# Pinning the side loads and sums of the adaLN weights in their written order, and moving all matmul operands to multiples of 256 bytes

## The chip, the cores and the metric

One core of a Trainium2 chip runs one program. The metric is the device time of the whole kernel in microseconds (us), median of three runs. Engines: PE (TensorE, matrix products), DVE (VectorE), ACT (ScalarE), POOL (GpSimd) and SP, which here only issues transfers from HBM. Each engine runs its own row of instructions strictly in order and waits on semaphores for the others. TensorE's clock is granted at one of two levels, 2.4 GHz (shown as 1.00) or 1.2 GHz.

## What is computed

Two layers over 512 positions of width 1024 (one sequence). Layer 0 is retention (4 heads, 64-position chunks), layer 1 is chunked attention (16 heads). Cut to what matters here:

```python
cond = silu(c)
for i in range(2):
    mod = cond @ ada_w[i] + ada_b[i]                 # 1024 -> 3072
    shift, scale, gate = split(mod, 3)
    h = rms_norm(x, norm_g[i]) * (1 + scale) + shift
    out = retention(h) if i == 0 else attention(h)   # projections in and out of the mixer
    x = x + gate * out
```

So `shift` and `scale` of layer 0 are needed before its first projection, its `gate` before the first output projection, and all of layer 1's `mod` only when layer 0 is over.

## The kernel before, in words

**Matrix products.** All operands are 4-byte values. Every operand of a large product is held as two parts, `hi` and `lo` (`hi` by ACT, `lo = raw - hi` by DVE), and each product is three matmuls, hi*hi, hi*lo and lo*hi: lines 231 to 233 (`nat_mm`) and 239 to 241 (`tr_mm`). Most are 128x128 stationary against 512 moving columns. A projection is a `Chunk` of 512 output columns: it loads two halves of 512 weight rows (1 MB, `raw`, two buffers), splits them (`whi`, `wlo`, two buffers each), and runs four units of 12 matmuls per half. Of the stationary operand and the moving one, one is a slice of the weight tiles, the other a slice of `hT` (the normed input), or, in an output projection (`po_r`, `po_a`), of the tiles `yh`, `yl`.

**The adaLN vectors.** `cond @ ada_w` is not done on PE: the weights come transposed, a block of 128 output features is a 128x1024 tile, and DVE multiplies it with `cond` and sums along the row (`ada_dot`, line 124; its trace name is CUSTOM_DVE_ANT_0). Shift and scale of layer 0 (16 blocks) are done in the first stage by `ada_256`. The other 32 blocks, 8 for layer 0's gate and 24 for layer 1, are called **side blocks**: `side_load` (line 589, 512 KB each, into two buffers of tag `ada`) and `side_dot`. The program hangs them on units of the projections: the first eight every second unit, the rest every third or fourth unit, the load four units ahead of its sum. When four sums are there, `ada_finish` adds the bias, and for the gate spreads it with two small PE products (`gp`) into `gates`, which POOL multiplies into the output weights (line 219).

**What sets the order.** The code is traced in the order written, but a scheduler then lays out each engine's row: an instruction whose inputs are early may move ahead of others. Side loads and sums have few inputs, so it moves them forward. The names used below: `rv`, `rqk`, `rg` are layer 0's projections for values, queries and keys, and the SiLU gate; `vl`, `ql`, `kl` low parts made from PSUM; `rt` rotary products; `st` scores, `ro` their product with the values, `ss` transposes for the norm of `ro`, which need `sq` summed by POOL (line 550); `dec` the decay table, loaded through POOL's queue; `ang`, `n` the rotary angles.

**Addresses.** Each tile has a fixed byte offset in every partition. In the built program before, the weight tiles `whi`, `wlo` and the tiles `hTh`, `hTl` start 128 bytes past a multiple of 256; `yh`, `yl` of most output projections, `qh`, `kh`, `pth`, `vh` and their low parts start at multiples of 256. So 2,736 of the 512-column matmuls take both operands at 128 past, 720 take one at 128 past and one at a multiple (384 of `po_r`, 288 of the first three `po_a`, 48 of the first half of `aqk0`), and the products of scores and values take both at multiples. The last output projection (`po_a` with `yh_last`) has both at 128 past.

Of the kernel before, what the change touches and what calls it, by code (L numbers as in the profile page):

```python
# [11 lines left out]
F32 = mybir.dt.float32  # L12
# [3 lines left out]
ALU = mybir.AluOpType  # L16

P = 128
S = 512
D = 1024  # L20
# [22 lines left out]
def hybrid_trunk_kernel(  # L43
# [20 lines left out]
    nc = tc.nc  # L64
    PS = bass.MemoryType.PSUM

    cp = ctx.enter_context(tc.tile_pool(name="cp", bufs=1))
# [3 lines left out]
    sp = ctx.enter_context(tc.tile_pool(name="sp", bufs=4))  # L71
# [20 lines left out]
    nc.vector.memset(ones, 1.0)  # L92
    ones_r = cp.tile([P, P], F32R, name="ones_r")
    nc.vector.tensor_copy(ones_r, ones)
    mhalf = cp.tile([P, 8], F32, name="mhalf")
    nc.gpsimd.memset(mhalf, -0.5)

    with tc.high_priority():
# [15 lines left out]
    def rstd_of(ss, n, w):  # L114

        ms = sp.tile([P, w], F32, tag="ms", name="ms")
        nc.gpsimd.tensor_scalar(ms, ss, 1.0 / n, EPS, ALU.mult, ALU.add)
        rs = sp.tile([P, w], F32, tag="rs", name="rs")
        nc.gpsimd.tensor_tensor(rs, ms, mhalf[:, :w], ALU.pow)
        return rs  # L120


    def ada_dot(raw, layer, block):
        nc.vector.tensor_tensor_reduce(  # L124
            raw, raw, cond, 1.0, 0.0, ALU.mult, ALU.add, mod[:, layer, block : block + 1]
        )

    def ada_finish(layer, b0, n):

        m, b = mod[:, layer, b0 : b0 + n], bt[:, layer, b0 : b0 + n]  # L130
        if b0 < NK:
            nc.vector.tensor_tensor(sh[:, layer, b0 : b0 + n], m, b, ALU.add)
            return
        nc.vector.tensor_tensor(m, m, b, ALU.add)
        if b0 < 2 * NK:
            g0 = b0 - NK
            nc.vector.scalar_tensor_tensor(
                gs[:, layer, g0 : g0 + n], m, 1.0, ng[:, layer, g0 : g0 + n], ALU.add, ALU.mult
            )
            return  # L140

        ps = pa.tile([P, n, P], F32, tag="pa", name=f"gp_{layer}_{b0}")
        for j in range(n):
            diag = np_.tile([P, P], F32, tag="diag", name=f"diag_{layer}_{b0 + j}", bufs=2)
            nc.vector.tensor_scalar(diag, ident, m[:, j : j + 1], None, ALU.mult)
            nc.tensor.matmul(ps[:, j, :], ones, diag, start=True, stop=True)
        g0 = (b0 - 2 * NK) * P
        nc.scalar.activation(
            gates[layer][:, g0 : g0 + n * P], ps.rearrange("p a b -> p (a b)"), AF.Copy
        )  # L150
# [12 lines left out]
    def norm_rows(t, tag, scalar=False):  # L163

        xn, ss = [], sp.tile([P, 2], F32, tag="ss", name=f"ss_{tag}_{t}")
        for half in range(2):
            xh = np_.tile([P, 512], F32, tag="p", name=f"xn_{tag}_{t}_{half}", bufs=6)
            nc.scalar.activation(
                xh, xs[t][:, half * 512 : (half + 1) * 512], AF.Square,
                accum_out=ss[:, half : half + 1],  # L170
            )
            xn.append(xh)
        s1 = sp.tile([P, 1], F32, tag="s1", name=f"s1_{tag}_{t}")
        nc.vector.tensor_tensor(s1, ss[:, 0:1], ss[:, 1:2], ALU.add)
        rs = rstd_of(s1, D, 1)
        for half in range(2):
            src = xs[t][:, half * 512 : (half + 1) * 512]
            if scalar:
                nc.scalar.activation(xn[half], src, AF.Copy, scale=rs)
            else:  # L180
                nc.vector.tensor_scalar(xn[half], src, rs, None, ALU.mult)
        return xn

    def norm_tile(layer, t):
        xn = norm_rows(t, layer)
        tsl = slice(t * P, (t + 1) * P)
        for half in range(2):
            ps = pa.tile([P, 4, P], F32, tag="pa", name=f"hp_{layer}_{t}_{half}")
            for k in range(4):
                nc.tensor.transpose(ps[:, k, :], xn[half][:, k * P : (k + 1) * P], ident)  # L190
            h = np_.tile([P, 4, P], F32, tag="nat", name=f"h_{layer}_{t}_{half}")
            for k in range(4):
                kt = half * 4 + k
                g1, s1 = gs[:, layer, kt : kt + 1], sh[:, layer, kt : kt + 1]
                if half == 0:
                    nc.vector.tensor_scalar(h[:, k, :], ps[:, k, :], g1, s1, ALU.mult, ALU.add)
                else:
                    nc.scalar.activation(h[:, k, :], ps[:, k, :], AF.Identity, bias=s1, scale=g1)
            ksl = slice(half * 4, half * 4 + 4)
            nc.scalar.activation(hT["h"][:, ksl, tsl], h, AF.Copy)  # L200
            nc.vector.tensor_tensor(hT["l"][:, ksl, tsl], h, f32(hT["h"][:, ksl, tsl]), ALU.subtract)
# [146 lines left out]
    with tc.tile_pool(name="st", bufs=1) as st:  # L348
        xT = st.tile([P, NK, S], F32, name="xT")

        def ada_256(b0):
            raw = st.tile([P, 2, D], F32, tag="ada", name=f"ada_0_{b0}", bufs=6)
            nc.sync.dma_start(
                raw, ada_t[0, b0 * P : (b0 + 2) * P, :].rearrange("(b p) k -> p b k", p=P)
            )
            for j in range(2):
                ada_dot(raw[:, j, :], 0, b0 + j)
            ada_finish(0, b0, 2)

        def norm_x():  # L360
            for t in range(NT):
                nc.sync.dma_start(xs[t], x[t * P : (t + 1) * P, :])
            for t in range(NT):
                xn = norm_rows(t, 0, t == 3)
                for half in range(2):
                    ps = pa.tile([P, 4, P], F32, tag="pa", name=f"hp_0_{t}_{half}")
                    for k in range(4):
                        nc.tensor.transpose(ps[:, k, :], xn[half][:, k * P : (k + 1) * P], ident)
                    nc.scalar.activation(
                        xT[:, half * 4 : half * 4 + 4, t * P : (t + 1) * P], ps, AF.Copy  # L370
                    )
# [42 lines left out]
    with ExitStack() as l0:  # L414
# [171 lines left out]

        def side_load(layer, block):
            raw = np_.tile([P, D], F32, tag="ada", name=f"ada_{layer}_{block}", bufs=2)
            nc.sync.dma_start(raw, ada_t[layer, block * P : (block + 1) * P, :])
            held[layer, block] = raw  # L590

        def side_dot(layer, block):
            ada_dot(held.pop((layer, block)), layer, block)
            if block % 4 == 3:
                ada_finish(layer, block - 3, 4)

        held = {}
        blocks = [(0, 16 + b) for b in range(8)]
        blocks += [(1, b) for b in (*range(8, 16), *range(8), *range(16, 24))]
        for z, (layer, block) in enumerate(blocks):  # L600
            u = 2 + 2 * z if z < 8 else 20 + (z - 8) * 7 // 2
            at(max(u - 4, 0), side_load, layer, block)
            at(u, side_dot, layer, block)
# [300 lines left out]
```

## Time and profile before

| What | Value |
|---|---|
| Time, median of 3 runs | 1009.23 us (1007.08 to 1010.11) |
| Time of the profiled execution | 1008.13 us |
| Its span, first to last instruction | 1006.4 us |
| PE busy | 961.0 us (95%) |
| DVE busy | 595.7 us (59%) |
| ACT busy, POOL busy | 373.1 us (37%), 183.5 us (18%) |
| Mean granted clock of PE over the span | 0.980 |

How to read it: PE is busy nearly all the time, so its row is the kernel's length wherever it does not wait; the share over the span hides that the first fifth is another stage. The profile's windows show, for a stretch of time, each engine's busy time, the granted clock of PE, and what the DMA engines moved. The list of waits says who waited for whom. A timeline row is start, length, engine, line, operation, output and inputs, count, and in brackets the idle time of that engine just before it and what ended it. A matmul's length in the trace includes its way through the array, so matmuls that follow each other overlap; what counts is the distance of their starts.

### The profile page before, as it was taken

How to read it: one execution, taken by the hardware profiler on the slowest of the kernel's cores; microseconds unless marked ns; L12 is line 12 of the kernel's file. 1: busy time of each engine (PE TensorE's matmuls, PEld its weight loads, DVE VectorE, ACT ScalarE, POOL GpSimd, SP SyncE). 2: the span in 40 equal slices, each digit the busy share in tenths (PEclk: the TensorE clock that was granted, in tenths of full speed). 3: DMA queues.
4: the chain of work that ended last, by engine and by line, in shares of the span. 5: the costliest groups of instructions: out<-in, count | busy, mean ns of one | idle time of the engine just before them, and what ended most of it. 6: DMA issues, size and time to landing. Idle time of an engine off the chain costs nothing.

```text
span 1006.4 us, 11781 instructions
## 1 busy us (share of the span) xinstructions
PE 961.0 (95%) x4528; PEld 800.4 (80%) x4528; DVE 595.7 (59%) x1023; ACT 373.1 (37%) x785; POOL 183.5 (18%) x169
## 2 busy tenths in 40 slices
PE   3879978999999999999999999999999999999997
PEld 2657766888888888888788888888888888888886
DVE  5989879435742474577345465735467346556674
ACT  6223222223222332426443454325534244543441
POOL 3000222006000203331200152002330012104410
PEclk8889988999999999999999999999999999999999
DMA  9868662231223122232133322232323231232202
GB/s 350 307 199 294 226 188 78 95 106 63 84 95 119 49 84 84 84 126 84 40 107 95 95 95 85 63 103 76 95 78 111 85 94 58 81 95 95 95 1 84
DMA packets 70296, 111.76 MB, mean 111 GB/s; under 512 B 11888, under 2 KB 36512, under 8 KB 70240
## 3 DMA queue, kind: packets, MB, share of 16 engines
q1 hardware_dynamic: 58256, 103.29, 30.7%
q0 software_dynamic: 10832, 5.62, 2.0%
q10 hardware_dynamic: 1152, 2.10, 0.6%
q8 instruction: 35, 0.57, 0.2%
q14 instruction: 21, 0.17, 0.0%
HBM read 108.83 MB, written 2.10 MB: 110 GB/s over the span
## 4 chain that ended last, share of the span: by engine, by line
PE 82%; DVE 10%; DMA 5%; issue 1%; ACT 1%; POOL 1%; SPq 0%; DVEq 0%; POOLq 0%
PE pm_aqk L231 6%; PE pm_aqk L233 6%; PE pm_aqk L232 6%; DVE ada L124 4%; DMA ada<-in_ada_t_dram 4%; PE as L723 3%; PE ao L763 3%; PE po_a L231 3%; PE po_a L233 3%; PE po_a L232 3%; PE pm_av L231 3%; PE pm_av L232 3%; PE pm_av L233 3%; PE po_r L231 3%; PE po_r L232 3%; PE po_r L233 3%
## 5 line engine op out<-in xcount | busy, mean ns | idle before, releaser
L231 PE MATMUL pm_aqk<-whi_aqk,hTh 128*128 128x512 f32 x256 | 102.0, 399 | 0.0
L233 PE MATMUL pm_aqk<-whi_aqk,hTl 128*128 128x512 f32 x256 | 100.5, 393 | 0.0
L232 PE MATMUL pm_aqk<-wlo_aqk,hTh 128*128 128x512 f32 x256 | 100.4, 392 | 0.0
L124 DVE CUSTOM_DVE_ANT_0 ada<-ada,cond 128x1024 f32<-128x1024 f32 x48 | 62.7, 1328 | 12.6 <-DMA ada<-in_ada_t_dram 12.6
L219 POOL TENSOR_TENSOR raw_r<-raw_r,gate 128x2048 f32<-128x2048 f32 x8 | 38.0, 4750 | 142.1 <-DMA raw_r<-in_ret_w_out_dram 89.3
L223 DVE TENSOR_TENSOR wlo_aqk<-raw_aqk,whi_aqk 128x2048 fp32r<-128x2048 f32 x16 | 41.0, 2562 | 30.4 <-ACT whi_aqk L222 30.4
L231 PE MATMUL pm_rv<-whi_rv,hTh 128*128 128x512 f32 x128 | 51.7, 409 | 7.6 <-ACT hTh L306 4.0
L233 PEld LDWEIGHTS pm_aqk<-whi_aqk,hTl 128*128 128x128 f32 x256 | 48.1, 188 | 10.2
L239 PE MATMUL pm_rqk<-hTh,whi_rqk 128*128 128x512 f32 x128 | 52.1, 411 | 4.2 <-DVE vl L307 4.2
L231 PEld LDWEIGHTS pm_aqk<-whi_aqk,hTh 128*128 128x128 f32 x256 | 48.1, 188 | 9.6
L232 PEld LDWEIGHTS pm_aqk<-wlo_aqk,hTh 128*128 128x128 f32 x256 | 48.2, 188 | 9.2
L231 PE MATMUL po_r<-whi_r,yh 128*128 128x512 f32 x128 | 51.4, 404 | 4.1 <-DVE x L327 4.1
L732 ACT ACTIVATE p<-p,nm 128x128 f32<-128x128 f32 (+1 forms) x64 | 35.9, 563 | 49.5 <-DVE nm L730 48.4
L241 PE MATMUL pm_rqk<-hTh,wlo_rqk 128*128 128x512 f32 x128 | 50.9, 403 | 2.3 <-DVE wlo_rqk L223 2.3
L240 PE MATMUL pm_rqk<-hTl,whi_rqk 128*128 128x512 f32 x128 | 52.2, 408 | 0.0
L726 DVE CUSTOM_DVE_ANT_0 p<-as,br 128x128 f32<-128x128 f32 (+1 forms) x64 | 30.4, 486 | 36.8 <-PE as L723 33.7
L232 PE MATMUL po_r<-wlo_r,yh 128*128 128x512 f32 x128 | 51.4, 402 | 0.0
L233 PE MATMUL po_r<-whi_r,yl 128*128 128x512 f32 x128 | 51.4, 401 | 0.0
L232 PE MATMUL pm_rv<-wlo_rv,hTh 128*128 128x512 f32 x128 | 50.8, 397 | 0.0
L239 PE MATMUL pm_ag<-hTh,whi_ag 128*128 128x512 f32 x128 | 50.7, 398 | 0.0
L711 POOL DMA_DIRECT2D br<-in_att_bias_dram x16 | 13.4, 839 | 203.7 <-DVE nm L730 168.5
L240 PE MATMUL pm_ag<-hTl,whi_ag 128*128 128x512 f32 x128 | 50.5, 394 | 0.0
(199 smaller groups left out, 2544.3 us busy)
## 6 DMA issues: line engine op xcount, KB each, us to landing
ada<-in_ada_t_dram SPq DMA_DIRECT2D x32, 512.0 KB, 4.6
raw_aqk<-in_att_w_in_dram SPq DMA_DIRECT2D x32, 512.0 KB, 4.7
ada<-in_ada_t_dram SPq DMA_DIRECT2D x8, 1024.0 KB, 14.1
raw_rg<-in_ret_w_in_dram SPq DMA_DIRECT2D x8, 1024.0 KB, 5.1
raw_r<-in_ret_w_out_dram SPq DMA_DIRECT2D x8, 1024.0 KB, 5.0
raw_ag<-in_att_w_in_dram SPq DMA_DIRECT2D x8, 1024.0 KB, 5.3
raw_av<-in_att_w_in_dram SPq DMA_DIRECT2D x8, 1024.0 KB, 5.3
raw_a<-in_att_w_out_dram SPq DMA_DIRECT2D x8, 1024.0 KB, 5.1
```

The source lines that it names most:

```text
L124: nc.vector.tensor_tensor_reduce(raw, raw, cond, 1.0, 0.0, ALU.mult, ALU.add, mod[:, layer, block : block + 1])
L219: nc.gpsimd.tensor_tensor(raw, raw, scale.unsqueeze(1).broadcast_to([P, k1 - k0, width]), ALU.mult)
L223: nc.vector.tensor_tensor(lo, raw, f32(hi), ALU.subtract)
L231: nc.tensor.matmul(ps, a_h, wh[:, k, :], start=first and k == 0, stop=False)
L232: nc.tensor.matmul(ps, a_h, wl[:, k, :], start=False, stop=False)
L233: nc.tensor.matmul(ps, a_l, wh[:, k, :], start=False, stop=last and k == 3)
L239: nc.tensor.matmul(ps, wh[:, k, csl], h, start=first and k == 0, stop=False)
L240: nc.tensor.matmul(ps, wh[:, k, csl], l, start=False, stop=False)
L241: nc.tensor.matmul(ps, wl[:, k, csl], h, start=False, stop=last and k == 3)
L723: nc.tensor.matmul(ps[:, :w0], a[:, qsl], b[:, :w0], start=z == 0, stop=z == 2)
L726: nc.vector.tensor_tensor_reduce(p[:, :w], ps[:, :w], br[:, S - w :], 1.0, -3.0e38, ALU.add, ALU.max, mx)
L732: nc.scalar.activation(p[:, :w], p[:, :w], AF.Exp, bias=nm, accum_out=sm)
```

## The change

Three kinds of lines change. `keep_in_program_order` adds an edge, without a semaphore, from the instruction that was traced just before on the same engine: the side load may not be placed ahead of the transfer written before it on SP, the side sum not ahead of the DVE instruction written before it. Other instructions remain free to move past them. Two small tiles are made larger, `mhalf` (8 to 40 columns) and `s1` (1 to 16 columns, of which column 0 is used); what lies behind them in a partition moves by 128 bytes. In the built program every matmul operand then starts at a multiple of 256 bytes.

```diff
-    mhalf = cp.tile([P, 8], F32, name="mhalf")
+    mhalf = cp.tile([P, 40], F32, name="mhalf")
...
     def ada_dot(raw, layer, block):
-        nc.vector.tensor_tensor_reduce(
+        return nc.vector.tensor_tensor_reduce(
             raw, raw, cond, 1.0, 0.0, ALU.mult, ALU.add, mod[:, layer, block : block + 1]
         )
...
-        s1 = sp.tile([P, 1], F32, tag="s1", name=f"s1_{tag}_{t}")
-        nc.vector.tensor_tensor(s1, ss[:, 0:1], ss[:, 1:2], ALU.add)
-        rs = rstd_of(s1, D, 1)
+        s1 = sp.tile([P, 16], F32, tag="s1", name=f"s1_{tag}_{t}")
+        nc.vector.tensor_tensor(s1[:, 0:1], ss[:, 0:1], ss[:, 1:2], ALU.add)
+        rs = rstd_of(s1[:, 0:1], D, 1)
...
         def side_load(layer, block):
             raw = np_.tile([P, D], F32, tag="ada", name=f"ada_{layer}_{block}", bufs=2)
-            nc.sync.dma_start(raw, ada_t[layer, block * P : (block + 1) * P, :])
+            tc.keep_in_program_order(
+                nc.sync.dma_start(raw, ada_t[layer, block * P : (block + 1) * P, :])
+            )
             held[layer, block] = raw

         def side_dot(layer, block):
-            ada_dot(held.pop((layer, block)), layer, block)
+            tc.keep_in_program_order(ada_dot(held.pop((layer, block)), layer, block))
             if block % 4 == 3:
                 ada_finish(layer, block - 3, 4)
```

The instructions are the same, but their order on every engine changes in layer 0. First place: DVE's row up to the first `vl`, the low part of the values, which frees the PSUM tile that PE needs for `rqk_2`. `ada_20` to `ada_22` are side blocks. Before:

```order
L436 TENSOR_SCALAR n_468<-ang 128x512
L124 ISA ada_21_740,mod<-ada_21_740,cond 128x1024
L124 ISA mod 128x1
L437 TENSOR_SCALAR n_468<-n_468 128x512
L439 SCALAR_TENSOR_TENSOR ang<-n_468,ang 128x512
L124 ISA ada_22_799,mod<-ada_22_799,cond 128x1024
...
L439 SCALAR_TENSOR_TENSOR ang<-n_468,ang 128x512
L307 TENSOR_TENSOR vl_491<-pm_rv_0_277,vh_490 128x512
```

With the change, the same place on DVE:

```order
L307 TENSOR_TENSOR hTl_112<-h_7_401,hTh_111 128x512
L429 CAST posf<-posi 128x512
L431 TENSOR_SCALAR ang<-posf,tiny 128x512
L436 TENSOR_SCALAR n_468<-ang 128x512
L437 TENSOR_SCALAR n_468<-n_468 128x512
L439 SCALAR_TENSOR_TENSOR ang<-n_468,ang 128x512 x2
L440 TENSOR_SCALAR n_469<-ang 128x512
L307 TENSOR_TENSOR vl_491<-pm_rv_0_277,vh_490 128x512
```

No side sum stands ahead of the first `vl` any more; the first, `ada_16`, comes after the fourth `vl`. Before, seven of them stood ahead of it, and all 32 ahead of the last `ql` of the second head; with the change the 32 are spread over DVE's row up to the fourth head. On ACT the two parts of `whi_rv_1` moved from behind the `hTh` of `h_4` and `h_5` to ahead of both.

Second place: SP's row of loads where the gate projection `rg` of the first head begins. Before:

```order
L589 DMA ada_20_674<-in_ada_t_dram 128x1024
L589 DMA ada_21_740<-in_ada_t_dram 128x1024
L589 DMA ada_22_799<-in_ada_t_dram 128x1024
L589 DMA ada_23_873<-in_ada_t_dram 128x1024
L589 DMA ada_8_1006<-in_ada_t_dram 128x1024
L589 DMA ada_9_1069<-in_ada_t_dram 128x1024
L214 DMA raw_rg_0_638<-in_ret_w_in_dram 128x4x512
L589 DMA ada_10_1155<-in_ada_t_dram 128x1024
L214 DMA raw_rg_1_753<-in_ret_w_in_dram 128x4x512
```

With the change, SP at the same place:

```order
L590 DMA ada_16_567<-in_ada_t_dram 128x1024
L590 DMA ada_17_569<-in_ada_t_dram 128x1024
L214 DMA raw_rqk_2_1_587<-in_ret_w_in_dram 128x4x256
L214 DMA raw_rg_0_638<-in_ret_w_in_dram 128x4x512
L590 DMA ada_18_585<-in_ada_t_dram 128x1024
L214 DMA raw_rg_1_753<-in_ret_w_in_dram 128x4x512
L214 DMA raw_rqk_0_897<-in_ret_w_in_dram 128x4x256 x2
L590 DMA ada_19_636<-in_ada_t_dram 128x1024
```

Ten side loads stood ahead of the first `rg` load; now two do, and later side loads stand singly or in twos and threes between the weight loads.

Third place: POOL's row at the end of the first head. Before:

```order
L219 TENSOR_TENSOR raw_r_0_1102<-raw_r_0_1102,gate_109 128x2048
L506 DMA dec_1123<-in_decay_dram 128x1x512
L507 MEMSET dec_1123 64x64
L550 TENSOR_TENSOR sq_814<-sq_814,sq_1_849 128x512
L550 TENSOR_TENSOR sq_814<-sq_814,sq_2_888 128x512
L550 TENSOR_TENSOR sq_814<-sq_814,sq_3_930 128x512
```

With the change:

```order
L506 DMA dec_1123<-in_decay_dram 128x1x512
L219 TENSOR_TENSOR raw_r_0_1102<-raw_r_0_1102,gate_109 128x2048
L507 MEMSET dec_1123 64x64
L550 TENSOR_TENSOR sq_814<-sq_814,sq_1_849 128x512
L550 TENSOR_TENSOR sq_814<-sq_814,sq_2_888 128x512
L550 TENSOR_TENSOR sq_814<-sq_814,sq_3_930 128x512
```

The load of the second head's decay table is issued ahead of the gate multiply instead of behind it; the three `sq` sums stand behind the `MEMSET`, which waits for that load, in both.

## Rows read from the trace of the kernel before

**Rows 1.** Windows: stretch, length, busy time of PE to POOL, granted clock, DMA share, GB/s

```profile
42.00:63.60 21.60, 18.01 (x74) 14.40 (x72) 18.94 (x41) 8.47 (x13) 2.19 (x5) 0.92 0.58 178
63.60:90.00 26.40, 19.92 (x75) 15.49 (x74) 23.68 (x38) 6.14 (x5) 0.15 (x1) 0.81 0.78 269
90.00:135.70 45.70, 43.77 (x215) 36.78 (x215) 37.84 (x59) 14.04 (x21) 5.94 (x2) 1.00 0.66 220
135.70:163.50 27.80, 17.42 (x70) 13.83 (x69) 27.80 (x39) 6.91 (x7) 12.05 (x6) 0.84 0.41 134
163.50:186.40 22.90, 22.87 (x96) 18.89 (x97) 16.27 (x24) 4.62 (x7) 0.88 (x1) 0.89 0.30 94
186.40:460.00 273.60, 273.60 (x1277) 228.97 (x1276) 140.11 (x157) 86.72 (x105) 51.35 (x27) 1.00 0.26 87
460.00:1006.40 546.40, 539.90 (x2626) 451.19 (x2624) 301.55 (x609) 227.85 (x592) 102.06 (x107) 1.00 0.26 83
```

**Rows 2.** Waits of PE, 0 to 180 us: total us, times, longest

```profile
PE ss L157 <- POOL sq L550: 6.3, 1, 6.3
PE pm_rqk L239 <- DVE vl L307: 4.2, 1, 4.2
...
PE pm_rv L231 <- ACT whi_rv L222: 3.6, 1, 3.6
```

**Rows 3.** The page's group of the sums, and two of DVE's timeline

```profile
L124 DVE CUSTOM_DVE_ANT_0 ada<-ada,cond 128x1024 f32<-128x1024 f32 x48 | 62.7, 1328 | 12.6 <-DMA ada<-in_ada_t_dram 12.6
...
59.39 1.23 DVE L124 CUSTOM_DVE_ANT_0 ada<-ada,cond 128x1024 f32<-128x1024 f32 x1 [2.29 <-DMA ada<-in_ada_t_dram]
...
67.36 1.28 DVE L307 TENSOR_TENSOR vl<-pm_rv,vh 128x512 fp32r<-128x512 f32 x2
```

**Rows 4.** Timeline of ACT at the gap of 42 us

```profile
43.85 1.15 ACT L306 ACTIVATE hTh<-h 128x512 fp32r<-128x512 f32 x2 [10.34 <-DVE h L379]
44.91 1.99 ACT L222 ACTIVATE whi_rv<-raw_rv 128x1024 fp32r<-128x1024 f32 x2
```

**Rows 5.** Timeline of POOL ahead of the wait of `ss`

```profile
125.15 0.84 POOL L506 DMA_DIRECT2D dec<-in_decay_dram  x1 [2.74 <-DVE pf L525]
136.55 0.14 POOL L507 MEMSET dec<- 64x64 f32 x1 [10.56 <-DMA dec<-in_decay_dram]
136.77 5.62 POOL L550 TENSOR_TENSOR sq<-sq,sq 128x512 f32<-128x512 f32 x3
```

**Rows 6.** DVE and POOL where POOL multiplies the gate, and the page's group of POOL

```profile
118.21 5.29 DVE L124 CUSTOM_DVE_ANT_0 ada<-ada,cond 128x1024 f32<-128x1024 f32 x1 [0.27 <-DMA ada<-in_ada_t_dram]
...
117.31 5.10 POOL L219 TENSOR_TENSOR raw_r<-raw_r,gate 128x2048 f32<-128x2048 f32 x1 [52.50 <-DVE ptl L307]
...
L219 POOL TENSOR_TENSOR raw_r<-raw_r,gate 128x2048 f32<-128x2048 f32 x8 | 38.0, 4750 | 142.1 <-DMA raw_r<-in_ret_w_out_dram 89.3
```

**Rows 7.** Groups of PE from 186 us on, forms apart: busy us, mean ns of one

```profile
L233 PE MATMUL po_r<-whi_r,yl 128*128 128x512 f32 x97 | 38.4, 396 | 0.0
...
L233 PE MATMUL pm_rv<-whi_rv,hTl 128*128 128x512 f32 x96 | 37.5, 390 | 0.0
...
L232 PE MATMUL po_a<-wlo_a,yh_last 128*128 128x512 f32 x30 | 11.7, 390 | 0.0
...
L540 PE MATMUL ro<-pth,vh 128*128 128x512 f32 x12 | 4.8, 400 | 0.0
L540 PE MATMUL ro<-ptl,vh 128*128 128x512 f32 x12 | 4.7, 390 | 0.0
```

**Rows 8.** Timeline of PE, at either level of its clock

```profile
32.04 1.07 PE L233 MATMUL pm_rv<-whi_rv,hTl 128*128 128x512 f32 x4
...
74.37 0.63 PE L239 MATMUL pm_rqk<-hTh,whi_rqk 128*128 128x512 f32 x1
74.80 0.63 PE L240 MATMUL pm_rqk<-hTl,whi_rqk 128*128 128x512 f32 x1
```

**Rows 9.** DMA issues of the page: count, KB each, median us to landing

```profile
ada<-in_ada_t_dram SPq DMA_DIRECT2D x32, 512.0 KB, 4.6
```

## The prediction

> **What bounds the kernel now.** I read the busy time by windows first [rows 1]. From 186.4 to 460 us PE is busy 273.60 of 273.60 us at clock 1.00: nothing on the other engines is worth anything there, only the length of the matmuls is. Between 42 and 186.4 us PE is not the bound. Its idle time is 21.60 − 18.01 = 3.6, 26.40 − 19.92 = 6.5, 45.70 − 43.77 = 1.9, 27.80 − 17.42 = 10.4 and 22.90 − 22.87 = 0: together 22.4 us. The idle time is paid twice, since after it PE runs at a granted clock below 1.00. If a share s of a window runs at the lower level, its mean clock is 1 − s/2, so the time at the lower level is 2(1 − clock) x window: 3.5, 10.0, 8.9 and 5.0 us (0.92, 0.81, 0.84, 0.89), 27.4 in all. Some of that is itself idle: in the first and the fourth window the idle time alone covers it, which leaves at least 10.0 − 6.5 and 5.0, together 8.5 us of work at the lower level; at most it is 27.4. A 512-column matmul follows the one before by 74.80 − 74.37 = 0.43 us at the lower level, and by (1.07 − 0.39)/3 = 0.227 us at the upper (a row of four less the length of one) [rows 8], so work at the lower level loses 47% of its time: 4.0 to 12.9 us, of which I take the middle, 8.5. What could be had back is 22.4 + 8.5 = **30.9 us**.
>
> Then I looked who it waits for [rows 2]: `ss` for POOL's `sq` (6.3), `pm_rqk` for DVE's `vl` (4.2), `pm_rv` for ACT's `whi_rv` (3.6). In the same windows DVE is busy 18.94 of 21.60, 23.68 of 26.40 and 27.80 of 27.80 us [rows 1]. Much of that are the side sums: 62.7/48 = 1.3 us each with 12.6 us of waiting for their loads [rows 3], and the order before has seven of them ahead of the first `vl`. The sum at 59.39 us ended a 2.29 us wait for its load while `vl`, at 67.36, stood behind it [rows 3].
>
> **The change part by part.**
>
> *Sums leave the front of DVE's row.* Nothing is added or removed: 32 sums at 1.22 us (an undisturbed one took 1.23 [rows 3]) stay 39 us of DVE. What PE still waits for afterwards I work out place by place from the new order.
> - Gap at 42 us. DVE has four sums ahead of `h_4` in both orders, so `h_4` comes no earlier. But ACT, which did `hTh` (1.15 for two) and then `whi_rv` (1.99 for two) [rows 4], now does `whi_rv` first, in the 10.34 us in which it was idle. PE needs one `whi_rv` and one `hTh` to go on: before it had them at 44.91 + 1.99/2 = 45.9 us, now at 43.85 + 1.15/2 = 44.4. So 1.5 of the 3.6 us go, 2.1 stay, and about 1 of lower clock.
> - Gap at 63.6. `vl` follows its PSUM tile at once and is there before PE asks; the 4.2 us go. What is late next is the low weight part of `rqk_2`, behind one load and two `vl`: 0.7 us stay.
> - `ss` at the end of the first head. It waited for POOL: the `dec` load was issued at 125.15, the MEMSET that waits for it started at 136.55, and three `sq` took 5.62 [rows 5]: 17.0 us in a row. The load is now issued ahead of POOL's gate multiply (5.10 us [rows 6]), which runs in its shadow. PE's row holds 42 long matmuls in between, 42 x 0.227 = 9.5 us, and 48 of `ro` with 320 columns in the mean, 48 x 0.227 x 320/512 = 6.8: 16.3 us. Nearly a tie: 0.7 us stay, 0 to 1.5.
> - `po_r` of the first head. POOL's second gate multiply stands by the `ql`, `kl` and rotary sums of DVE. A DVE operation with two inputs in SBUF was held by such a multiply: the sum at 118.21 took 5.29 us, 4.07 more than 1.22, while POOL's ran from 117.31 for 5.10 [rows 6]. So 0 to 4.1 us stay here, take 2.
>
> Sum: 3.1 + 0.7 + 0.7 + 2 = 6.5 us stay, and 30.9 − 6.5 = **24.4 us** are won. The ends: 22.4 + 4.0 − (3.1 + 0.7 + 1.5 + 4.1) = 17, and 22.4 + 12.9 − (3.1 + 0.7) = 31.5.
>
> *Where the sums go.* 24 of them, 24 x 1.22 = 29 us, land where DVE is busy 140.11 of 273.60 us [rows 1], 62% with them. PE's slack covers a plain sum, since weights are split a chunk ahead. What it may not cover is a sum or another DVE operation that POOL holds: six of POOL's eight gate multiplies (38.0 us [rows 6]) lie behind 186 us, each a chance to hold one by 4.07. I take 1 us of cost and 0 to 8 as bounds. From 460 us on the rows are the same in both.
>
> *Loads.* With two buffers, load k waits in SP's row for sum k − 2, and weight loads queue behind it. In the new order the sum that releases it stands on DVE ahead of the weight split that frees the next weight buffer at nearly every place, so the weight load would wait for DVE anyway: 0 (the cover is that PE waits for no weights behind 186 us [rows 1]; without it see the fourth rival).
>
> *Operands at multiples of 256.* 720 matmuls of 512 columns had operands on different sides of the 256-byte grid. `po_r` (128 and 0) has a mean length of 396 ns, `pm_rv` (both 128) 390, the last `po_a` (both 128) 390, `ro<-ptl,vh` (both 0) 390 [rows 7]. So equal sides are what counts, by 6 ns: 720 x 6 ns = **4.3 us** won. Bounds: 0, if the 6 ns belong to `po_r` for another reason; and, since I don't see why equal sides should help, 9 us either way of my number from the one deviating row with both at 0: `ro<-pth,vh` has 400 [rows 7], and if a third of the 2,736 matmuls that move from 128 to 0 took 10 ns more, 9 us would be lost.
>
> A page speaks against this part. The rows show 396 beside 390 ns for the same shape [rows 7]. The Trainium skill, "SBUF — State Buffer", section "SBUF: two separate sides", says that of the engines only DVE and GpSimd contend for a port and that PE never waits on anyone; by it an address would cost nothing, and the 4.3 us would be 0. So far the row decides, and the rule is the first rival.
>
> **Sum.** The profiled execution took 1008.13 us; 1008.1 − 24.4 − 4.3 + 1 = 980.4 us. The median of the runs shown is 1.1 us above it: **981.5 us**.
>
> **The rivals.**
> - *The addresses give nothing.* For it: the matmuls of `po_r` also differ by their PSUM and by who reads it. Against it: `yh_last` has the same consumers with 390 ns. Time 981.5 + 4.3 = 986.
> - *Collisions with POOL reach PE.* The spread sums are the DVE operations that a gate multiply holds longest, and the weight splits stand behind them. All six behind 186 us at 4.07 give 24 us: 981.5 − 1 + 24 = 1005. For it: the sum at 118.21 [rows 6]. Against: before, such operations stood there too, without one wait of PE.
> - *TensorE gains by every matmul.* If the 128-byte offset, whatever the other operand's, is what makes the distance 227 ns [rows 8] instead of 512 columns at 2.4 GHz = 213, then 3,456 matmuls x 14 ns = 48 us go: 981.5 + 4.3 − 48 = 938. Against: the rows with both at 0 show 390 ns, not less [rows 7]. The Trainium skill, "TensorE: Matmul & The Clock Gate", section "Wait — 56ns, not 53.3ns?", has 215.7 ns for 512 columns, which is 11 ns under this kernel's distance; no run here shows it.
> - *Slower: pinned side loads starve the weights.* If at a side block behind 186 us the weight load waits in SP's row until the block's load is released, PE loses up to a load's landing, 4.6 us [rows 9]. The gain of 24.4 + 4.3 us is gone from 28.7/24 = 1.2 us per block. Half a landing at each of 24 is 55 us: 981.5 + 55 = 1037. Against: the order of DVE above, and two weight buffers of a chunk each.
> - *The change doesn't do what it says.* The order shows the sums spread, but if the stalls came from the loads' bandwidth instead, all of it but the 4.3 us stays: 1005 or above. Against: DMA share is 0.58 to 0.78 in the windows [rows 1], and the waits name DVE and POOL [rows 2].
>
> **How the numbers follow.** Chances: forecast 0.70, addresses give nothing 0.13, collisions 0.07, starved weights 0.05, not doing what it says 0.03, gain by every matmul 0.02. The forecast's own range is 972 to 993, from the ends of the early gain (7.1 us more, 7.4 less) together with part of the address bounds. It contains the first rival; the rivals outside hold 0.17. Within 0.3% (3 us), about what a measurement of this kernel can tell from no change, or slower, lie only the last ends of collisions and the case that nothing moves. So: range **972 to 994**; faster 0.91, within 0.3% 0.04, slower 0.05.
>
> **What would show it.** Right: PE idle between 46 and 186 us nearly gone and its clock at 1.00 there; the first `pm_rg` some 11 us earlier; the wait of `ss` under 1 us; the second head's first `pm_rv` some 25 us earlier; side sums up to about 400 us; `po_r` at 390 ns. Wrong: waits of PE for `wlo` or `whi` of any weight behind 160 us (collisions or starved loads; a DMA named there means loads); `po_r` still at 396 (addresses); `pm_rv` at another length than 390 (the bound on the 0 side).

## The result: 984.3 us, 25.4 us less, nearly all of it ahead of the second head

| | before | changed |
|---|---|---|
| Time, median | 1009.67 us (1007.08 to 1013.84) | 984.29 us (982.59 to 985.68) |
| Ratio, 95% interval | | 0.9744 (0.9705 to 0.9783) |
| Span of the profiled execution | 1006.4 us | 981.2 us |
| Mean granted clock | 0.980 | 0.992 |

The forecast was 981.5 us, with a range of 972 to 994. The windows of the changed kernel over the same stretches as [rows 1] (stretch, length, busy time of PE, PEld, DVE, ACT and POOL, granted clock, DMA share, GB/s):

```profile
42.00:63.60 21.60, 18.93 (x76) 15.24 (x76) 17.09 (x36) 8.73 (x14) 2.59 (x6) 0.92 0.39 122
63.60:90.00 26.40, 24.06 (x106) 19.95 (x107) 22.16 (x30) 8.70 (x10) 0.00 (x0) 1.00 0.61 211
90.00:135.70 45.70, 45.70 (x234) 39.23 (x233) 34.38 (x54) 15.88 (x21) 13.85 (x8) 1.00 0.44 138
135.70:163.50 27.80, 27.80 (x131) 23.32 (x130) 26.20 (x33) 8.69 (x9) 5.42 (x2) 1.00 0.49 158
163.50:186.40 22.90, 22.90 (x103) 18.96 (x102) 10.25 (x12) 6.12 (x6) 0.14 (x1) 1.00 0.41 142
186.40:460.00 273.60, 270.99 (x1280) 227.03 (x1279) 174.20 (x220) 94.73 (x147) 57.90 (x34) 1.00 0.35 117
```

Of the 22.4 us in which PE was idle between 42 and 186 us, 2.67 + 2.34 = 5.0 are left, and the clock is 1.00 from 63.6 us on, where it was 0.81, 0.84 and 0.89 in three of four windows. PE's waits say the same (total us, times, longest). The first two lines are of the stretch up to 180 us, the others from there on:

```profile
PE pm_rv L231 <- ACT hTh L306: 6.7, 2, 4.0
PE pm_rqk L241 <- DVE wlo_rqk L223: 2.5, 1, 2.5
...
PE pt L745 <- DVE p L737: 2.0, 2, 1.1
PE qt L671 <- DVE qn L663: 1.2, 1, 1.2
PE pm_aqk L231 <- ACT hTh L200: 1.1, 1, 1.1
PE gp L146 <- DVE diag L145: 1.1, 1, 1.1
PE po_r L231 <- ACT whi_r L222: 0.5, 1, 0.5
```

The waits of [rows 2] for `sq` and `vl` are gone, `wlo_rqk` and the gap of 42 us (2.7 of the 6.7 for `hTh`; the other 4.0 is at 23 us, in both kernels) remain, and four small waits have come behind 390 us: `pm_aqk`, `gp`, `po_r` and one of the two of `pt`, 1.1 + 1.1 + 0.5 + 1.1 = 3.8 us. The start of the second head's first `pm_rv` sums up the early part. Before, on PE's timeline:

```profile
186.44 0.39 PE L231 MATMUL pm_rv<-whi_rv,hTh 128*128 128x512 f32 x1
```

and with the change:

```profile
159.28 0.39 PE L231 MATMUL pm_rv<-whi_rv,hTh 128*128 128x512 f32 x1
```

PE has done the same number of matmuls up to here in both. So 27.2 us were won up to here; the end shows 25.2 (the two spans). What the addresses gave behind this point was more than eaten by the new waits. On the page, the group of the sums that answers to [rows 3] waits 1.7 us for its loads, not 12.6, and the sums cost the same:

```profile
L124 DVE CUSTOM_DVE_ANT_0 ada<-ada,cond 128x1024 f32<-128x1024 f32 x48 | 63.3, 1332 | 1.7 <-DMA ada<-in_ada_t_dram 1.7
```

### The profile page after: what moved, and what is told of

Its sections match the earlier page's. It is cut to its first block, busy times and chain, and to the rows that moved or that the text cites. A ratio compares the mean times of both kernels' runs of the same rounds, so it can differ in the third digit from the quotient of the medians.

```text
span 981.2 us, 11783 instructions
## 1 busy us (share of the span) xinstructions
PE 949.3 (97%) x4528; PEld 793.6 (81%) x4528; DVE 601.1 (61%) x1023; ACT 373.8 (38%) x785; POOL 184.7 (19%) x169
## 4 chain that ended last, share of the span: by engine, by line
PE 86%; DMA 4%; issue 4%; DVE 3%; ACT 1%; POOL 1%; SPq 0%; POOLq 0%; ACTq 0%; DVEq 0%
PE pm_aqk L233 5%; PE pm_aqk L231 5%; PE pm_aqk L232 5%; PE po_a L231 3%; PE po_a L233 3%; PE po_a L232 3%; PE pm_av L232 3%; PE pm_av L233 3%; PE pm_rg L239 3%; PE pm_rg L240 3%; PE ao L765 3%; PE as L725 3%; PE pm_av L231 3%; PE pm_rg L241 3%; PE ro L540 3%
## 5 line engine op out<-in xcount | busy, mean ns | idle before, releaser
L223 DVE TENSOR_TENSOR wlo_aqk<-raw_aqk,whi_aqk 128x2048 fp32r<-128x2048 f32 x16 | 36.6, 2290 | 28.0 <-ACT whi_aqk L222 28.0
L241 PE MATMUL pm_ag<-hTh,wlo_ag 128*128 128x512 f32 x128 | 50.2, 395 | 0.0
L231 PE MATMUL pm_av<-whi_av,hTh 128*128 128x512 f32 x128 | 50.0, 391 | 0.0
```

The lines of the kernel that those rows point to most:

```text
L223: nc.vector.tensor_tensor(lo, raw, f32(hi), ALU.subtract)
L231: nc.tensor.matmul(ps, a_h, wh[:, k, :], start=first and k == 0, stop=False)
L241: nc.tensor.matmul(ps, wl[:, k, csl], h, start=False, stop=last and k == 3)
```

## Experiments

### The two parts apart

`align_only` is the kernel before with only the two tiles enlarged; the rows of all engines stay in their order.

```diff
-    mhalf = cp.tile([P, 8], F32, name="mhalf")
+    mhalf = cp.tile([P, 40], F32, name="mhalf")
...
-        s1 = sp.tile([P, 1], F32, tag="s1", name=f"s1_{tag}_{t}")
+        s1 = sp.tile([P, 16], F32, tag="s1", name=f"s1_{tag}_{t}")
```

> The kernel before with the two larger tiles alone: the same rows on every engine, all operands at multiples of 256. Theory (operands on different sides of the 256-byte grid cost about 5 ns each): `po_r` and the first three `po_a` fall from 395-402 to 391-398 ns, the loss of 720 such matmuls, 3 to 4.3 us, goes, and nothing else: 1009.7 - 3.5 = about 1006 us. Rival (the lengths of `po_r` came from something else and fell in the changed kernel with the order): 1009.7 us and `po_r` at 395 ns.

Measured: 1005.39 us, ratio 0.9955 (0.9941 to 0.9969), so 3.1 to 6.0 us less. PE's early waits are the old ones (`sq` 6.5, `vl` 4.4 us), and `po_r` is at 391 ns. `edges_only` is the other part alone:

```diff
-    mhalf = cp.tile([P, 40], F32, name="mhalf")
+    mhalf = cp.tile([P, 8], F32, name="mhalf")
...
-        s1 = sp.tile([P, 16], F32, tag="s1", name=f"s1_{tag}_{t}")
+        s1 = sp.tile([P, 1], F32, tag="s1", name=f"s1_{tag}_{t}")
```

> The changed kernel with the two tiles at their old sizes: its order, the addresses of before. Theory (the order brings the early gain, the addresses the rest): `po_r` back at 395 ns and about 3 us above the changed kernel's 984.3: 987 us. Rival (addresses give nothing): 984.3 us.

Measured: 989.36 us, 0.9798 (0.9774 to 0.9822), 5 us above the changed kernel, where 3 were expected; `po_r` is back at 395 to 396 ns. Its profiled execution has longer waits, `pt` 3.5 us and `gp` 1.7, against 2.0 and 1.1, which can account for the other two; that is argued from one execution, of 991.06 us, and not shown. So the addresses give about 4 us and the order 20, and the two add up.

### Sides or multiples

In `mixed` the order is the changed kernel's, but a spare 128-byte tile stands between the pool of `hT` and that of the weights, and `s1` is small again. `hT`, `yh` and `yl` start at multiples of 256, the weights 128 past.

```diff
+    gap = ctx.enter_context(tc.tile_pool(name="gap", bufs=1))
     wp = ctx.enter_context(tc.tile_pool(name="wp", bufs=2))
...
+    spare = gap.tile([P, 32], F32, name="spare")
+    nc.gpsimd.memset(spare, 0.0)
```

> The changed kernel's order, but the weight tiles moved by 128 bytes and nothing else of the large products: `hT`, `yh` at multiples of 256, `whi`, `wlo` 128 past, so 3,408 matmuls of 512 columns take their operands from different sides. Theory (different sides cost 5 to 6 ns): 17 to 20 us above the changed kernel, 1001 to 1005 us, `pm_rv` at 395 ns. Rival (only `po_r` and `po_a` are slow, for their PSUM or their readers): 984 us. Second rival (an operand 128 past costs something by itself): the kernel before, with both 128 past, would have shown it too, 984 us here plus whatever it costs there, 0 by its 390 ns.

Measured: 999.09 us, 0.9892 (0.9866 to 0.9918): 14.8 us above the changed kernel, a little less than the 17 to 20 expected, or 14.8/3,408 = 4.3 ns for each matmul that changed sides. `at128` is the mirror: every operand 128 past.

```diff
-    mhalf = cp.tile([P, 40], F32, name="mhalf")
+    mhalf = cp.tile([P, 8], F32, name="mhalf")
```

> The changed kernel's order with every operand of the 512-column products 128 bytes past a multiple of 256: equal sides, none at a multiple. Theory (equal sides count, not the multiple): 984.3 us within a microsecond, `pm_rv` and `po_r` at 390 to 391 ns. Rival (multiples of 256 count): slower by 3,456 matmuls times what one costs, 17 us at 5 ns.

Measured: 985.77 us, 0.9764 (0.9743 to 0.9784), no difference from the changed kernel that these runs can tell. Groups of PE from 186 us on (busy us, mean ns of one), first of `mixed`:

```profile
L241 PE MATMUL pm_rg<-hTh,wlo_rg 128*128 128x512 f32 x94 | 37.1, 395 | 0.0
L240 PE MATMUL pm_rg<-hTl,whi_rg 128*128 128x512 f32 x93 | 36.7, 395 | 0.0
```

then of `at128`:

```profile
L232 PE MATMUL po_r<-wlo_r,yh 128*128 128x512 f32 x96 | 37.5, 391 | 0.0
...
L240 PE MATMUL pm_rg<-hTl,whi_rg 128*128 128x512 f32 x91 | 35.5, 390 | 0.0
```

`pm_rg`, which has equal sides before the change and after it, goes from 390 to 395 ns when its weights move by 128 bytes; `po_r`, 395 to 396 with one operand at a multiple and one 128 past, goes to 391 with both 128 past. The other products with weights show the like in `mixed`. So it is the sides that count. That the operands stand at multiples of 256, as the change says of itself, is not what helps.

### Which edge does it

`sums_pinned` has the edges on the sums alone, `loads_pinned` on the loads alone.

```diff
-            tc.keep_in_program_order(
-                nc.sync.dma_start(raw, ada_t[layer, block * P : (block + 1) * P, :])
-            )
+            nc.sync.dma_start(raw, ada_t[layer, block * P : (block + 1) * P, :])
```

> The changed kernel with the edges on the sums alone; the loads are free. With two buffers load k cannot start ahead of sum k - 2, so SP's row comes out nearly as in the changed kernel: two side loads ahead of the first `rg` load. Theory (what counts is DVE's row): 984.3 us within 2. Rival (SP's row counts, the pinned loads keep the weight loads in time): some of the 25 us is lost again, 990 us or more.

Measured: 981.27 us, 0.9716 (0.9695 to 0.9737). That is 3.0 us below the changed kernel, where the theory allowed 2; the two intervals overlap. With the sums in place the edges on the loads are worth nothing that can be measured. In this trace the wait for `wlo_rqk` is gone, and one of 3.9 us for `wlo_rv` has come.

```diff
-            tc.keep_in_program_order(ada_dot(held.pop((layer, block)), layer, block))
+            ada_dot(held.pop((layer, block)), layer, block)
```

> The edges on the loads alone; the sums are free, and the scheduler places three of them ahead of the first `vl` (before: seven; changed: none), and all 32 in DVE's row end about halfway between the two kernels. SP: four side loads ahead of the first `rg` load (before ten, changed two). Theory (each sum at the front of DVE's row costs its 1.2 us and its load's wait): between the two, 990 to 1000 us, with PE waiting for `vl` or `wlo_rqk` at 63 us. Rival (SP's row alone decides): 984 to 987 us.

Measured: 986.21 us, 0.9767 (0.9747 to 0.9787), and neither theory is right about it: the time lies in the rival's range (984 to 987 us), but the place of the theory is there. The place where three sums stand ahead of `vl` loses what the theory says. DVE's timeline there:

```profile
62.51 1.23 DVE L124 CUSTOM_DVE_ANT_0 ada<-ada,cond 128x1024 f32<-128x1024 f32 x1 [2.50 <-DMA ada<-in_ada_t_dram]
63.66 0.08 DVE L124 DVE_READ_ACCUMULATOR2_ANT mod<- 128x1 f32 x1
63.66 0.69 DVE L307 TENSOR_TENSOR vl<-pm_rv,vh 128x512 fp32r<-128x512 f32 x1
```

A sum that waits 2.50 us for its load keeps `vl` until 63.66; PE waits 4.1 us for `vl` and 2.1 for `wlo_rqk`, as before. But it has no wait for `sq`, one of 1.3 us for `ptl`, and none of the new ones for `gp`, `po_r` and `pm_aqk`. My mistake was to price the row as a whole, halfway between the kernels: only the sums that stand ahead of something PE waits for cost anything. Either edge brings the later sums back far enough: the last one starts at 160 us before the change, at 385 with it, at 384 with the sums pinned and at 342 with the loads pinned. Since with two buffers loads and sums hold each other, these two runs don't part DVE's row from SP's row of loads; what names DVE's row is PE's waits, `vl` behind a sum above all.

### What the spread sums still cost

`no_mult` leaves out POOL's gate multiplies.

```diff
-        if scale is not None:
+        if False:
             nc.gpsimd.tensor_tensor(
```

> The changed kernel without POOL's gate multiplies of the output weights (left out in both layers, so the gates are not applied). The changed kernel has new PE waits behind 186 us: `gp` for a diagonal that DVE took 4.80 us for while POOL multiplied, `po_r` for `whi_r` behind a multiply, `pt` for a `p` held 4.72 us: 1.1 + 0.5 + 1.1 us and the restart, about 3.1 us. Theory (POOL's multiplies hold DVE): these waits are gone, 981 us; `hTh` at the layer's end (1.3 us) stays. Rival (the spread sums are late by themselves): the waits stay, 984 us.

Measured: 977.76 us, 0.9684 (0.9667 to 0.9701), 6.5 us below the changed kernel, twice what was expected. The waits for `gp` and `whi_r` are gone, and `hTh` of layer 1 and all of `pt` with them, which I had not put down to POOL. In the changed kernel, DVE and POOL at `gp`, then at `pt` (of the two `diag` in the first line, the longer took 4.58 us):

```profile
393.69 4.80 DVE L145 TENSOR_SCALAR diag<-ident,mod 128x128 f32<-128x128 f32 x2
...
393.83 4.58 POOL L219 TENSOR_TENSOR raw_r<-raw_r,gate 128x2048 f32<-128x2048 f32 x1 [9.92 <-DMA raw_r<-in_ret_w_out_dram]
...
711.23 4.58 POOL L219 TENSOR_TENSOR raw_a<-raw_a,gate 128x2048 f32<-128x2048 f32 x1 [2.91 <-DVE ri L736]
...
711.25 4.72 DVE L737 TENSOR_SCALAR p<-p,ri 128x256 f32<-128x256 f32 x1
```

The kernel before has the same two instructions of layer 1 in the same order on either engine:

```profile
736.74 0.35 DVE L735 TENSOR_SCALAR p<-p,ri 128x256 f32<-128x256 f32 x1
...
736.96 4.62 POOL L219 TENSOR_TENSOR raw_a<-raw_a,gate 128x2048 f32<-128x2048 f32 x1 [3.15 <-DVE ri L734]
```

There DVE began 0.22 us ahead of POOL and took 0.35 us; here POOL began 0.02 us ahead, DVE took 4.72, and PE waited 1.1 us. So it hangs on a coincidence: in `at128`, whose DVE and PE rows have the changed kernel's order, a `p` was held from 580 to 584 us (4.41 us), and none at 711. Such hits may be part of the spread of 982.6 to 985.7 us between runs of one kernel; that was not tested.

### The wait that stayed

`posi_early` loads the positions into a tile that is unused until later, so that DVE can do the angles sooner.

```diff
-            posi = np_.tile([P, S], I32, tag="nat", name="posi")
+            posi = gates[1][:, 0:S].bitcast(I32)
```

> The changed kernel with one more change: the positions are loaded into the second gate tile, which is unused until much later, instead of into a buffer that the normed input must free first, so the load is issued at the start instead of at 50.7 us, and DVE does the angles from 51 us on instead of from 55.7. Theory (the 2.5 us that PE waits for `wlo_rqk_2` come from the angles being late, since the split stands behind four `vl` and them): that wait and about 0.3 us of its restart go, 981.5 us. Rival (the split is late for its load or for ACT's `whi_rqk_2`): 984 us, the wait stays or moves to `whi_rqk`.

Measured: 989.40 us, 0.9798 (0.9776 to 0.9820), slower than the changed kernel. Neither theory had this. The wait for `wlo_rqk` stayed (3.4 us), since a second small load, `tiny`, came at 56.6 us and the angles still waited. And a new wait of 3.2 us for `sq` came, for a reason that tests the third place of the change. POOL's timeline in this run:

```profile
104.55 0.81 POOL L506 DMA_DIRECT2D dec<-in_decay_dram  x1 [43.57 <-DVE pf L525]
114.45 0.15 POOL L507 MEMSET dec<- 64x64 f32 x1 [9.09 <-DMA dec<-in_decay_dram]
114.75 4.65 POOL L219 TENSOR_TENSOR raw_r<-raw_r,gate 128x2048 f32<-128x2048 f32 x1 [0.15 <-ACT yh L558]
119.35 5.28 POOL L550 TENSOR_TENSOR sq<-sq,sq 128x512 f32<-128x512 f32 x3
```

and in the changed kernel:

```profile
103.17 0.81 POOL L506 DMA_DIRECT2D dec<-in_decay_dram  x1 [41.63 <-DVE pf L525]
105.37 5.59 POOL L219 TENSOR_TENSOR raw_r<-raw_r,gate 128x2048 f32<-128x2048 f32 x1 [1.39 <-ACT gate L148]
113.04 0.15 POOL L507 MEMSET dec<- 64x64 f32 x1 [2.08 <-DMA dec<-in_decay_dram]
113.27 5.38 POOL L550 TENSOR_TENSOR sq<-sq,sq 128x512 f32<-128x512 f32 x3
```

The edit moved the multiply behind the `MEMSET`, so it no longer runs in the shadow of the load. The chain from issue to the last `sq` is 20.1 us instead of 15.5, and PE waits. `angles_early` gives `tiny` a place of its own too, and there the multiply is ahead of the `MEMSET` again:

```diff
+    tiny_c = cp.tile([P, 64], F32, name="tiny")
...
-            tiny = rp.tile([P, 64], F32, name="tiny")
+            tiny = tiny_c
```

> As the run with early positions, with the table of inverse frequencies in a place of its own too. In that run the angles still began at 56.6 us, because this second small load was issued at 49.97 us and landed then; so the wait it was to remove was not tested. Now both are there early, and DVE can do the angles from about 50.5 us on; POOL's row has the gate multiply again ahead of the `MEMSET` of the decay table. Theory (late angles hold `wlo_rqk_2`): the 2.5 us wait and its restart go, 981.5 us. Rival (the four `vl` alone hold it): the wait stays above 1.5 us, 983 us or more.

Measured: 983.13 us, 0.9734 (0.9717 to 0.9751). The wait for `wlo_rqk` is down to 0.3 us. But PE now waits 1.5 us for `whi_rqk` in its place, and its first instruction comes at 12.8 us instead of 9.7: POOL's row, where the two small loads now stand at the start, does its first `rs` (line 119) at 10.4 us instead of 8.6, behind a second `ms`. So the theory of the angles is right at its place, and nothing can be measured of it in the total.

### A faster version

`mult_dve` lets DVE multiply the gate; `angles_mult` is that and `angles_early`; `angles_mult0` is the same with DVE's multiplies in the first layer alone.

```diff
-            nc.gpsimd.tensor_tensor(
+            nc.vector.tensor_tensor(
                 raw, raw, scale.unsqueeze(1).broadcast_to([P, k1 - k0, width]), ALU.mult
```

> The changed kernel with the gate multiplies done by DVE instead of POOL (16 multiplies of about 2.3 us by the rows of the weight splits of the same size). Theory (POOL's multiplies cost by holding DVE, and 37 us more of DVE are covered): most of the 6.5 us that leaving them out gave, 978 to 981 us, no DVE operation over 2.5 us, no wait for `gp` behind 186 us. Rival (DVE's row is too full for them): new waits for `wlo` or `x`, 984 us or more.

Measured: 983.41 us, 0.9729 (0.9711 to 0.9746). The multiplies take 2.29 us each on DVE, no `diag` is held any more (283 ns in the mean instead of 552), and the four new waits behind 390 us are gone. But the second layer has another, 2.6 us of `po_a` for `qn`, and `wlo_rqk` cost 3.2 us in this execution. So the theory is right in what goes, and its 978 to 981 us are missed; the rival's full row showed in one place, though not in a wait for `wlo` or `x`.

> Both of the two changes above together. If both theories hold, the gains add: about 976 to 978 us. If only one holds, the time of that one.

Measured: 980.14 us, 0.9705 (0.9689 to 0.9720). That is 4.1 us below the changed kernel by the medians, where the two alone had 1.2 and 0.9, neither clear of noise, and it is above the 976 to 978 expected.

```diff
-            nc.vector.tensor_tensor(
+            (nc.vector if name[0] == "r" else nc.gpsimd).tensor_tensor(
                 raw, raw, scale.unsqueeze(1).broadcast_to([P, k1 - k0, width]), ALU.mult
```

> As the run with early angles and DVE's multiplies, but DVE multiplies the gate of the first layer alone (8 of the 16); in the second layer POOL does, as in the changed kernel. With all 16 on DVE the first layer lost nothing behind 80 us to `gp`, `po_r` or `hTh`, but the second had a new wait of 2.3 us of `po_a` for `qn` and lost some 4 us more there than the changed kernel. Theory (DVE has room in the first layer and none to spare in the second): about 3 us less than with all 16, 977 us. Rival (the second layer's small waits come and go by coincidence, with POOL's or with DVE's multiplies): 980 us, with `p` or `ptl` held in the second layer instead.

Measured: 979.01 us, 0.9699 (0.9683 to 0.9715). It has the lowest median of the complete versions, 5.3 us below the changed kernel's; but its interval still overlaps that of the changed kernel (0.9705 to 0.9783), and it can't be told from `angles_mult`. The rival has the detail right: `pt` waits 3.2 us in three places again, with `p` held by POOL's multiplies.

## Why the prediction was right

**Cause and place.** Side sums at the front of DVE's row held the steps that PE waited for. Pinning the sums alone gives the whole gain. The starved weights of the fourth rival did not come: no wait of PE behind 160 us names a DMA or a `wlo`. One of 0.5 us names a `whi`, which the prediction had listed as a sign of being wrong: `po_r` waited for `whi_r`, which stood behind POOL's multiply, and that is the collisions' side of the sign.

**What could be had back** was taken as 30.9 us and was more. The start of the second head's `pm_rv` moved by 27.2 us, 0.4 of it by the addresses of the first head's 96 `po_r`; 5.0 us of idle time with about 1.5 of slower clock are still there: near 33 us. The idle part, 22.4, was read off; so some 11 us were lost beside it, at the lower clock and in restarts. That is near the upper end of the bounds (4.0 to 12.9), not the middle, 8.5.

**What stays** was taken as 6.5 us and is about 6.5, but two terms were off and cancelled. For the gap at 42 us I said 2.1 us, and it is 2.7. The low weight part of `rqk_2` was given 0.7 us and costs 2.5. This step counted one load and two `vl`, and left out the angles that stand between the `vl`. DVE's timeline of the changed kernel:

```profile
62.26 0.68 DVE L307 TENSOR_TENSOR vl<-pm_rv,vh 128x512 fp32r<-128x512 f32 x1
62.86 0.68 DVE L443 SCALAR_TENSOR_TENSOR ang<-n,ang 128x512 f32<-128x512 f32 x1
63.46 0.68 DVE L307 TENSOR_TENSOR vl<-pm_rv,vh 128x512 fp32r<-128x512 f32 x1
64.06 0.68 DVE L444 SCALAR_TENSOR_TENSOR ang<-n,ang 128x512 f32<-128x512 f32 x1
64.66 1.22 DVE L223 TENSOR_TENSOR wlo_rqk<-raw_rqk,whi_rqk 128x1024 fp32r<-128x1024 f32 x1
```

Every other step is one of the angles. They began at 55.7 us, when the positions came, after DVE had waited 4.27 us for them, and `angles_early` shows that without this the split is there 2.2 us sooner for PE. Against that, `ss` and `po_r` of the first head wait 0 instead of 0.7 and 2. The multiply did run in the shadow of the load, and the chain came to 15.5 us, not 17.0. One sign missed by the same terms: the first `pm_rg` was to come some 11 us earlier and came 8.3 earlier, at 76.04 instead of 84.37 us.

**Addresses** were taken as 4.3 us. `align_only` has 3.1 to 6.0 by its interval; by the rows, 395 to 391 ns, it is 4 to 5 ns x 720 = 2.9 to 3.6. The first rival (nothing) falls with `mixed`: 14.8 us from the addresses alone. There the prediction also preferred the row to the rule of the Trainium skill, "SBUF — State Buffer", section "SBUF: two separate sides". The rule is on who waits for whom, and the runs show nothing against that; it just tells nothing of where an operand starts. The rival in which every matmul gains falls with `at128`: both operands 128 past are as fast as both at multiples. The bound of 9 us the other way did not come either: `pm_rv`, which moved from 128 to 0, stayed at 389 to 391 ns.

**The spread sums** were taken as 1 us, with 0 to 8 as bounds. It is 3.8 us of new waits and, by estimate, about 0.6 of restarts. The rival of collisions is thus true in its mechanism, at a sixth of its price: one `diag` at 393 us was held for 4.58, and PE saw 1.1 of it. The step that was too small is this 1 us. The prediction showed the hold on a sum, with two inputs in SBUF; `diag` and `p` read one tile and a column of factors, and they are held as long, just where PE waits for them at once. The trace of the kernel before has such a hold already, DVE and POOL in the second head:

```profile
155.04 4.83 DVE L145 TENSOR_SCALAR diag<-ident,mod 128x128 f32<-128x128 f32 x2
...
154.57 5.03 POOL L219 TENSOR_TENSOR raw_r<-raw_r,gate 128x2048 f32<-128x2048 f32 x1 [0.29 <-ACT gate L148]
```

Behind it in DVE's row stands, at 162.75 us, the `x` that PE waited 4.1 us for. So, by the rows, part of the early idle time was a collision too; no run tests it by itself. The Trainium skill, "SBUF — State Buffer", section "SBUF: two separate sides", names operations in a two-port mode beside those with two inputs in SBUF, each against a lock held for a whole instruction; the 4.58 and 4.72 us, beside POOL's 4.58, agree with that, though no row tells in which mode the two ran.

Put together, with the 624 of the 720 matmuls that lie behind the second head's `pm_rv` at 4 to 5 ns: 27.2 + 2.8 − 4.4 = 25.6 us, beside 25.2 between the spans. The forecast of 27.7 (24.4 + 4.3 − 1) was near partly by luck: an early gain that was too small and a later cost that was too small went against each other.

## What to carry to other kernels

- When an engine that is not the bound shows near 100% in one stretch and half that later, look at what its scheduler has moved to the front: work with few inputs runs ahead of the step that the bound waits for. An edge that only orders can bring it back; the edges on the sums were enough, and the loads followed.
- Price such a move place by place, with the row of everything that stands between the released step and its data. The term that was most off here had left out the steps of another chain in the same row.
- Let both operands of a matmul start at multiples of 256 bytes, or both 128 past; which one doesn't matter here, and other offsets were not run. And expect gains of this size to be blurred by a few us of coincidences between POOL and DVE.

## What had not been expected of the hardware

- A 512-column matmul of 4-byte values with one operand at a multiple of 256 bytes and the other 128 past took 4 to 5 ns more than the 227 of one with equal sides, in the kernel's products with weights (`pm_rg` 390 to 395 ns by a shift of its weights by 128 bytes). Why is open: no run here looks inside.
- POOL's multiply of 4.6 us held a DVE operation of 0.3 us that reads a single tile: `diag` took 4.58 us and `p` 4.72. In the two rows shown, which of the two started first decided: POOL 0.02 us ahead held `p`, DVE 0.22 us ahead took 0.35.
